# Four store buffers for layer 0's last latent tiles, and another start and pace for the row maxima of both layers

## The chip, the cores and the metric

The kernel runs on one core of one Trainium2 chip. The metric is the device time of one execution in microseconds (us), as the median of several runs. A profile of one further execution shows what every engine did: TensorE (PE, with its weight loads shown apart as PEld), VectorE (DVE), ScalarE (ACT), GpSimd (POOL), and the queues of DMAs, of which SP issues most.

## The reference

Two layers of a diffusion backbone over 2048 latent tokens and 256 context tokens (18 tiles of 128), width 1024, all in float32. Layer 0 is latent attention beside gated linear attention, layer 1 a 2-D neighbourhood attention over windows of 8 x 16 grid positions. Cut to what matters here:

```python
# layer 0 (even): one wide projection, then queries and keys out of low-rank latents
lat = split_cols(jnp.dot(h, w_in), EVEN_SPLITS)            # q_lat 768, kv_lat 256, k_rope 32, gates, B branch
q = rms_norm(rms_norm(q_lat) @ w_uq, q_gain); k = rms_norm([rms_norm(kv_lat) @ w_ukv, k_rope], k_gain)   # 8 heads x 96
o = softmax(q k^T * scale) v                                # over all tokens and the context
# layer 1 (odd): q, k, v, z = split(h @ w_in), 16 heads x 64
s_lat = q . k_window + bias;  s_ctx = q . k_ctx
p = softmax(concat([s_lat, s_ctx]));  y = (p v * silu(z)) @ w_out
```

Both softmaxes subtract a row maximum. The kernel computes these maxima in a pass of its own, ahead of the attention.

## The kernel before

Products are kept at float32 accuracy by splitting each operand into a high and a low part and adding three matmuls: one *step* of a product over the width is three matmuls, and a *cell* (one tile of 128 tokens by one block of weight columns) has eight steps.

The program is written as Python that traces instructions in an order of priority. A planner then puts them into the fixed order of each engine's queue, by its own estimate of times, of data dependences and of when buffers come free. `issue_after(x)` makes everything traced inside it stand behind instruction `x` on `x`'s engine. A tile is named by a tag, and the tag has a number of buffers; a new tile of the tag waits until the oldest one's last reader is done. Pools that are opened later take the space of pools that are closed, and each of their tiles waits for the readers of what lay there.

**Layer 0, latent tiles** (`even_latent`, L436 and on). A loop over 18 tiles runs, each with an offset: `prep` and `gemm` (latent projection), `up` (queries and keys out of the latents) and `fin` (L582 to L599). `fin` takes a tile's queries (`z` = 0) and keys (`z` = 1) in two halves `h2` of four heads: four transposes into a bank `tp`, then ACT writes the high part and DVE the low part into a tile `qkhl` with two buffers, and SP stores it to DRAM with three DMAs (L597 twice, L598 once). Beside it, `ada_steps` computes modulation rows with the tags `adac0`, `adac1` (one buffer each) and `adaw` (two buffers); its sixteen parts are used up before tile 14 comes to `fin`. During the last tiles, `first` already computes some cells of the next stage, and weights of the next stage are loaded (`wraw`, L422) and split (`W...`, `wr1`) on ACT and DVE.

**Layer 0, the rest of the projection** (`even_rest`). 86 cells, 688 steps, run from the last tile to the first. `maxes` runs beside them: for each of 8 heads it loads the keys (`mk`, L685 and L686) and queries (`mq`), multiplies and takes maxima with DVE (L698, L699). That is 664 pieces of side work. Two of the weights that the cells need are loaded and split in the first 32 steps.

`weave(main, side, ratio, lag, head)` interleaves the two: after `head` steps of main work it draws `ratio` pieces of side work per step, and each main step is put behind the side piece that is `lag` pieces back. So side work may fall behind by `lag` pieces, and no more:

```python
        due, done, over = -float(head * ratio), [], 0.0
                n = len(done) - lag - 1 + int(over)
                if n >= 0:
                    es.enter_context(self.tc.issue_after(done[min(n, len(done) - 1)].ins))
```

**Layer 1, values and gates** (`odd_vz`). 65 cells, 520 steps; beside them `maxes` for 16 heads of 16 query blocks each, 256 pieces: two matmuls into banks `mx` (five of them), POOL's two additions to a head's bias table `mtab`, and DVE's additions with a running maximum (L1689 to L1702). This `maxes` already loads its keys behind the last weight load (`wload`).

**Layer 1, attention** (`odd_attention`). Its loads are one chain on SP (`load`, L113: each behind the one before), in this order: queries of the odd head, first keys, values, two bias tables, context keys, queries of the even head (`q`, needed by the first scores), second keys, context values, mask, and so on. Their tiles lie in the space of the stage before: the first queries in that of `mk` and `mtab`, the values in that of `mtab`, the keys, tables and even queries in that of the last weights of `odd_vz`, the mask in that of its activations.

Of the kernel before, what the change touches and what calls it, by code (L numbers as in the profile page):

```python
# [10 lines left out]
F32 = mybir.dt.float32  # L11
F32R = mybir.dt.float32r
# [5 lines left out]
P = 128  # L18
# [5 lines left out]
NT = T // P  # L24
# [3 lines left out]
A_HEADS, A_NOPE, A_ROPE, A_V = 8, 64, 32, 64  # L28
A_QK = A_NOPE + A_ROPE
# [59 lines left out]
class Kern:  # L89
# [346 lines left out]
    def even_latent(self, ws, wrest, kept):  # L436
        nc, tc = self.nc, self.tc
# [5 lines left out]
        with ExitStack() as es:  # L443
# [3 lines left out]
            with ExitStack() as es2:  # L447
# [4 lines left out]
                hi, lo = win[0] = [self.tl(ws, [P, KD, LAT_CHUNK], "W0" + z, F32R, bufs=1) for z in "hl"]  # L452
# [8 lines left out]
            sp = self.pool(es, "esA", bufs=2, side="left", reuse_waits="tile")  # L461
# [120 lines left out]
            def fin(t):  # L582
                qn, kn = nat.pop(t)
                for z, (src, da, dc) in enumerate(((qn, self.QA, self.QC), (kn, self.KA, self.KC))):
                    col = 2 * z + (0 if t < NCT else 1)
                    for h2 in range(2):
                        ps = self.tl(pp, [P, 4, P], "tp")
                        for j in range(4):
                            nc.tensor.transpose(ps[:A_QK, j, :], src[:, h2 * 4 + j, :], self.ident[:])
                        hl = self.tl(sp, [P, 4, 2, P], "qkhl", F32R, bufs=2)  # L590
                        hi, lo = hl[:A_QK, :, 0, :], hl[:A_QK, :, 1, :]
                        self.act(hi, ps[:A_QK], AF.Copy, scale=qkg[:A_QK, col : col + 1])
                        nc.vector.scalar_tensor_tensor(out=lo, in0=ps[:A_QK], scalar=qkg[:A_QK, col : col + 1],
                                                       in1=hi, op0=ALU.mult, op1=ALU.subtract)
                        hs, ts = slice(h2 * 4, h2 * 4 + 4), slice(t * P, t * P + P)
                        for part in range(2):
                            nc.sync.dma_start(da[part, hs, :, ts].rearrange("h d t -> d h t"), hl[:A_NOPE, :, part, :].bitcast(F32))  # L597
                        nc.sync.dma_start(dc[hs, :, :, ts].rearrange("h s d t -> d (h s) t"),  # L598
                                          hl[A_NOPE:A_QK].rearrange("d h s t -> d (h s) t").bitcast(F32))  # L599

            ada = self.ada_steps([(0, 4), (0, 5)] + [(1, b) for b in range(6)], sp, pp, "tp")

# [39 lines left out]
    def even_rest(self, ws, win, hT):  # L642
        nc = self.nc
        self.zaT = self.scr("zaT", (4, P, T), F32)
        self.x1 = self.scr("x1", (T, D), F32)
        with ExitStack() as es:
            wp = self.pool(es, "ewB", side="left", reuse_waits="tile")
            sp = self.pool(es, "esB", bufs=2, side="left", reuse_waits="tile")
            pp = self.pool(es, "epB", bufs=2, space=PSUM, reuse_waits="tile")
            self.ahead += [self.held(self.rest_steps(win, 0, ws, "WU")), self.rest_steps(win, 1, wp, "wr1")]  # L650

            def cell(t, j):
                hi, lo = hT[t]
                wh, wl = win[j]
                w = self.REST[j]
                ps = self.tl(pp, [P, 512], "gm")
                yield from self.mm3_steps(ps[:, :w], (lambda k: hi[:, k, :], lambda k: lo[:, k, :]),
                                          (lambda k: wh[:, k, :], lambda k: wl[:, k, :]), range(KD))
                u = self.tl(sp, [P, 512], "u", bufs=4)
                if j < 2:  # L660
                    self.last_tanh = self.act(u[:], ps[:], AF.Tanh, scale=0.5)
                    nc.vector.scalar_tensor_tensor(out=u[:], in0=u[:], scalar=1.0, in1=ps[:], op0=ALU.add, op1=ALU.mult)
                else:
                    self.act(u[:, :w], ps[:, :w])
                if j == 0:
                    pt = self.tl(pp, [P, 4, P], "tp", bufs=1)
                    for b in range(4):
                        nc.tensor.transpose(pt[:, b, :], u[:, b * P : b * P + P], self.ident[:])
                    z = self.tl(sp, [P, 4, P], "zt")
                    self.act(z[:], pt[:])  # L670
                    nc.gpsimd.dma_start(self.zaT[:, :, t * P : t * P + P].rearrange("j p t -> p j t"), z[:])
                elif j == 1:
                    st = nc.gpsimd.dma_start(self.Un[t, :, 1056:], u[:])
                    with self.tc.issue_after(st.ins):
                        nc.gpsimd.dma_start(self.x1[t * P : t * P + P, :], self.i["xin"][t * P : t * P + P, :])
                else:
                    nc.gpsimd.dma_start(self.Un[t, :, (j - 2) * 352 : (j - 1) * 352], u[:, :352])

            cells = self.cells(list(range(NT))[::-1], (2, 3, 4, 0, 1), lambda t, j: j not in (2, 3) or t < NT - 2)
            gemms = self.stream(cells, hT, cell, lambda t: self.reload(0, t))  # L680

            def maxes():
                for h in range(A_HEADS):
                    k = self.tl(sp, [P, T], "mk", F32R, bufs=2)
                    nc.sync.dma_start(k[:A_NOPE].bitcast(F32), self.KA[0, h])  # L685
                    nc.sync.dma_start(k[A_NOPE:A_QK].bitcast(F32), self.KC[h, 0])  # L686
                    m = self.tl(sp, [P, NT, 5], "mm")
                    nc.vector.memset(m[:], -3e38)
                    for t in range(NT):
                        if t % 6 == 0:  # L690
                            q = self.tl(sp, [P, 768], "mq", F32R)
                            nc.sync.dma_start(q[:A_NOPE].bitcast(F32), self.QA[0, h, :, t * P : t * P + 768])
                            nc.sync.dma_start(q[A_NOPE:A_QK].bitcast(F32), self.QC[h, 0, :, t * P : t * P + 768])
                        lim = CTX if t < NCT else T
                        for n, k0 in enumerate(range(0, lim, 512)):
                            w = min(512, lim - k0)
                            ps = self.tl(pp, [P, 512], "mx", bufs=5)
                            mm = nc.tensor.matmul(ps[:, :w], q[:A_QK, (t % 6) * P : (t % 6) * P + P], k[:A_QK, k0 : k0 + w], start=True, stop=True)  # L698
                            nc.vector.tensor_reduce(out=m[:, t, n : n + 1], in_=ps[:, :w], axis=AX.X, op=ALU.max)  # L699
                            yield mm  # L700
                    mc = self.tl(sp, [P, NT], "mc", bufs=1)
                    nc.vector.tensor_reduce(out=mc[:], in_=m[:], axis=AX.X, op=ALU.max)
                    ps = self.tl(pp, [P, 512], "mx", bufs=5)
                    mm = nc.tensor.transpose(ps[:NT, :P], mc[:], self.ident[:])
                    r = self.tl(sp, [P, P], "mr", F32R, bufs=1)
                    self.act(r[:NT], ps[:NT, :P], AF.Copy, scale=-1.0)
                    nc.gpsimd.dma_start(self.QM[h].rearrange("(t p) -> t p", p=P), r[:NT].bitcast(F32))
                    yield mm

            self.weave(gemms, maxes(), 1.06, 30, 20)  # L710

    @staticmethod
    def back_order():
# [899 lines left out]
    def odd_vz(self, ws, win, hT):  # L1613
        nc = self.nc
# [3 lines left out]
        with ExitStack() as es:  # L1618
            sp = self.pool(es, "osB", bufs=2, side="left", reuse_waits="tile")
# [93 lines left out]
            first = [NT - 3, NT - 2, NT - 1]  # L1713
            cells = self.cells(first + list(range(NT - 3))[::-1], (4, 5, 6, 7), lambda t, j: (j > 4 or t < NT - 3) and (j < 6 or t >= NCT))
            gemms = self.stream(cells, hT, cell, lambda t: self.reload(1, t))
            self.weave(gemms, maxes(), 0.57, 15, 32)


    def odd_attention(self, out, right, left, wout):
# [508 lines left out]
```

## Time and profile before

| | |
|---|---|
| median of 3 runs | 3563.59 us (3560.05 to 3564.49) |
| the profiled execution | 3565.63 us, of which the span of its instructions 3563.9 us |
| mean granted PE clock | 0.984 |
| busy: PE, DVE, ACT, POOL | 97%, 68%, 41%, 35% of the span |
| moved by DMA | 526.75 MB, mean 148 GB/s |

A line of the profile's timeline has the start, the duration, the engine, the line of the program, the operation, what it writes from what it reads, and a count; at its end stands how long the engine was idle before it and what ended that. A row of the windows view has a stretch of time, its length, each engine's busy time with a count of instructions, the granted clock of PE as a share, the mean busy share of the DMA engines, and GB/s. Busy PE time is not PE at its peak: where the granted clock is 0.5, the same matmul takes about twice as long.

### The profile page before, as it was taken

To read this page: it belongs to the slowest core of one execution; us is meant where nothing else is said; L and a number is where in the kernel's file an instruction comes from. 1 tells how busy PE (TensorE), PEld (TensorE's weight loads), DVE (VectorE), ACT (ScalarE), POOL (GpSimd) and SP (SyncE) were. 2 spreads that over 40 slices of the span, in tenths; PEclk is the share of its full clock that TensorE was granted. 3 is DMA by queue.
4 is the path that set the end of the run, shared out by engine and by line. 5 is a ranking of instruction groups with operands and counts; after the bars stand their busy time and mean duration, and the time that the engine had idled before them with its cause. 6 is when DMAs were issued, how large, how long until landed. Compare 5 with 4: busy or idle time off the path is not lost. (4 is left out here: it accounts for less than half of the span.)

```text
span 3563.9 us, 54063 instructions
## 1 busy us (share of the span) xinstructions
PE 3453.2 (97%) x19460; PEld 2666.8 (75%) x19460; DVE 2431.0 (68%) x4798; ACT 1449.8 (41%) x2647; POOL 1243.9 (35%) x1400
## 2 busy tenths in 40 slices
PE   7999999999999999999999999999999997999999
PEld 6888987888896666665557878888788885556577
DVE  4677756888885777768876655444477874666875
ACT  5445542111113554546664354544322222555532
POOL 1333431111111333422211144334234443888852
PEclk9999999999999999999999999999999998999999
DMA  7555555232315242334525765445744447888684
GB/s 253 144 158 157 152 141 152 91 107 93 102 65 165 62 133 80 103 116 132 176 79 142 144 193 151 134 138 164 244 139 159 155 152 183 206 223 219 192 234 79
DMA packets 379596, 526.75 MB, mean 148 GB/s; under 512 B 34633, under 2 KB 254233, under 8 KB 372882
## 3 DMA queue, kind: packets, MB, share of 16 engines
q1 hardware_dynamic: 326450, 405.32, 39.3%
q0 software_dynamic: 29856, 82.14, 9.2%
q10 hardware_dynamic: 23024, 35.85, 3.0%
q8 instruction: 154, 2.52, 0.3%
q14 instruction: 112, 0.92, 0.1%
HBM read 344.39 MB, written 196.60 MB: 152 GB/s over the span
## 5 line engine op out<-in xcount | busy, mean ns | idle before, releaser
L699 DVE TENSOR_REDUCE mm<-mx 128x1 f32<-128x512 f32 (+1 forms) x656 | 388.3, 627 | 82.5 <-PE mx L698 75.5
L108 ACT ACTIVATE apt<-st 128x1024 f32<-128x1024 f32 (+1 forms) x296 | 300.0, 1014 | 313.2 <-PE st L1168 298.0
L1175 DVE TENSOR_TENSOR acc<-acc,apt 128x1024 f32<-128x1024 f32 x256 | 340.6, 1330 | 80.6 <-ACT apt L108 61.5
L1168 PE MATMUL st<-aq,akh 64*128 64x512 f32 x1728 | 313.9, 411 | 1.1 <-ACT apt L108 0.8
L1078 PE MATMUL av<-apt,av 128*64 128x512 f32 x1152 | 265.8, 598 | 0.0
L1945 DVE TENSOR_TENSOR opt<-st,tab 128x64 f32<-128x64 f32 (+10 forms) x576 | 144.2, 315 | 151.0 <-PE st L1787 67.6
L1826 POOL TENSOR_TENSOR oacc<-oacc,opt 128x576 f32<-128x576 f32 (+5 forms) x192 | 223.3, 1186 | 39.2 <-ACT rl L108 19.6
L698 PE MATMUL mx<-mk,mq 96*128 96x512 f32 (+1 forms) x656 | 236.0, 373 | 0.5 <-DVE mm L699 0.5
L1168 PE MATMUL st<-aq,akl 64*128 64x512 f32 (+1 forms) x1152 | 231.4, 393 | 0.0
L1702 DVE CUSTOM_DVE_ANT_1 mx<-mx,mtab 128x217 f32<-128x217 f32 (+12 forms) x576 | 183.6, 339 | 53.3 <-PE mx L1696 40.6
L108 ACT ACTIVATE u<-gm 128x352 f32<-128x352 f32 (+1 forms) x140 | 68.4, 496 | 370.9 <-PE gm L133 208.5
L1168 PEld LDWEIGHTS st<-aq,akh 64*128 64x128 f32 x1728 | 154.1, 187 | 83.6 <-ACT apt L108 28.0
L1078 PEld LDWEIGHTS av<-apt,av 128*64 128x64 f32 x1152 | 76.2, 136 | 135.3 <-issue 134.3
L108 ACT ACTIVATE opt<-opt 128x930 f32<-128x930 f32 (+8 forms) x130 | 104.5, 805 | 108.6 <-DVE opt L1945 104.2
L698 PEld LDWEIGHTS mx<-mk,mq 96*128 96x128 f32 x656 | 121.2, 188 | 12.9 <-DVE mm L699 1.6
L1168 PEld LDWEIGHTS st<-aq,akl 64*128 64x128 f32 (+1 forms) x1152 | 112.6, 186 | 24.2
L1691 DVE TENSOR_REDUCE mm<-mx 128x2 f32<-128x512 f32 x128 | 88.3, 690 | 46.1 <-PE mx L1689 45.0
L220 POOL TENSOR_TENSOR oss<-oss,mhalf 128x8 f32<-128x8 f32 x68 | 113.3, 1666 | 5.0
L131 PE MATMUL gm<-w1h,hhi 128*128 128x512 f32 x280 | 112.2, 401 | 0.0
L133 PE MATMUL gm<-w1h,hlo 128*128 128x512 f32 x280 | 110.3, 394 | 0.0
L1786 PE MATMUL st<-q,kt 128*128 128x480 f32 (+5 forms) x256 | 99.5, 391 | 11.1 <-DVE opt L1945 8.1
L132 PE MATMUL gm<-w1l,hhi 128*128 128x512 f32 x280 | 110.0, 393 | 0.0
(694 smaller groups left out, 9743.9 us busy)
## 6 DMA issues: line engine op xcount, KB each, us to landing
q<-Q SPq DMA_DIRECT2D x48, 512.0 KB
H<-x ACTq DMA_DIRECT2D x32, 512.0 KB
adaw<-ada_w SPq DMA_DIRECT2D x64, 256.0 KB
wraw<-w_od SPq DMA_DIRECT2D x64, 256.0 KB
K1t<-okt POOLq DMA_DIRECT2D x32, 512.0 KB, 10.1
kt<-K1t SPq DMA_DIRECT2D x32, 512.0 KB
x<-H SPq DMA_DIRECT2D x31, 512.0 KB
mtab<-rpb_q SPq DMA_DIRECT2D x16, 899.0 KB
```

Of the source, the lines that this page charges most:

```text
L108: return self.nc.scalar.activation(out, in_, func, **kw)
L131: self.nc.tensor.matmul(out, lh(k), rh(k), start=start and j == 0, stop=False)
L133: yield self.nc.tensor.matmul(out, ll(k), rh(k), start=False, stop=stop and j == n - 1)
L220: return g.tensor_tensor(out=out, in0=out, in1=self.mhalf[:, : shp[1]], op=ALU.pow)
L698: mm = nc.tensor.matmul(ps[:, :w], q[:A_QK, (t % 6) * P : (t % 6) * P + P], k[:A_QK, k0 : k0 + w], start=True, stop=True)
L699: nc.vector.tensor_reduce(out=m[:, t, n : n + 1], in_=ps[:, :w], axis=AX.X, op=ALU.max)
L1078: mm = nc.tensor.matmul(O[j, nb][i * 64 : i * 64 + 64, :w], V[j, kt // TT][:, kt % TT, i * 64 : i * 64 + 64], pts[:, i, :w], start=n == 0, ...
L1168: mm = nc.tensor.matmul(ps[:, o // 64, :w], k[o : o + r, kb, kq], Q[o : o + r, qb, :w], start=m == 0, stop=m == 4)
L1175: added = nc.vector.tensor_tensor(out=acc[:, :, :w], in0=a[:, :, :w], in1=pts[:, :, :w], op=ALU.add)
L1702: nc.vector.tensor_tensor_reduce(out=s, in0=s, in1=tb[:, ri : ri + rn, ci : ci + cn], scale=1.0, scalar=-3e38, op0=ALU.add, op1=ALU.max, a ...
L1826: self.psum = nc.gpsimd.tensor_tensor(out=a, in0=a, in1=pts[:, :, a0 - r0 : a1 - r0, :], op=ALU.add)
L1945: bias = nc.vector.tensor_tensor(out=pt[:, d[0], d[1]], in0=ps[:, d[0], d[1]], in1=tabs[j][i][:, ri : ri + rn, ci : ci + cn], op=ALU.add)
```

## The change

Three things are changed.

- In `fin`, for the tiles 14 to 17, the second half of the heads (`h2` = 1) no longer takes a `qkhl` buffer. Its two parts go to tiles of their own: for the queries (`z` = 0) `adac0` and `adac1`, for the keys (`z` = 1) the two buffers of `adaw`. The sizes are the same. Such a half is stored with four DMAs and not three, since its parts no longer lie beside each other.
- Layer 0's weave starts the maxima after 36 steps (20 before) at 1.09 pieces a step (1.06 before), with the same lag of 30. Each head's key loads stand behind the weight load traced last.
- Layer 1's weave draws 0.615 pieces a step (0.57 before), with the same lag of 15 and the same head of 32.

```diff
@@ fin, in even_latent
-                        hl = self.tl(sp, [P, 4, 2, P], "qkhl", F32R, bufs=2)
-                        hi, lo = hl[:A_QK, :, 0, :], hl[:A_QK, :, 1, :]
+                        if t < NT - 4 or h2 == 0:
+                            hl = self.tl(sp, [P, 4, 2, P], "qkhl", F32R, bufs=2)[:A_QK]
+                            hi, lo = hl[:, :, 0, :], hl[:, :, 1, :]
+                        else:
+                            tags = [("adaw", 2)] * 2 if z else [("adac0", 1), ("adac1", 1)]
+                            hi, lo = [self.tl(sp, [P, 4, P], a, F32R, bufs=n)[:A_QK] for a, n in tags]
...
-                        for part in range(2):
-                            nc.sync.dma_start(da[part, hs, :, ts].rearrange("h d t -> d h t"), hl[:A_NOPE, :, part, :].bitcast(F32))
-                        nc.sync.dma_start(dc[hs, :, :, ts].rearrange("h s d t -> d (h s) t"),
-                                          hl[A_NOPE:A_QK].rearrange("d h s t -> d (h s) t").bitcast(F32))
+                        for part, y in enumerate((hi, lo)):
+                            nc.sync.dma_start(da[part, hs, :, ts].rearrange("h d t -> d h t"), y[:A_NOPE].bitcast(F32))
+                            if t >= NT - 4 and h2:
+                                nc.sync.dma_start(dc[hs, part, :, ts].rearrange("h d t -> d h t"), y[A_NOPE:].bitcast(F32))
+                        if t < NT - 4 or h2 == 0:
+                            nc.sync.dma_start(dc[hs, :, :, ts].rearrange("h s d t -> d (h s) t"),
+                                              hl[A_NOPE:].rearrange("d h s t -> d (h s) t").bitcast(F32))
@@ maxes, in even_rest
-                    nc.sync.dma_start(k[:A_NOPE].bitcast(F32), self.KA[0, h])
-                    nc.sync.dma_start(k[A_NOPE:A_QK].bitcast(F32), self.KC[h, 0])
+                    with self.tc.issue_after(self.wload.ins):
+                        nc.sync.dma_start(k[:A_NOPE].bitcast(F32), self.KA[0, h])
+                        nc.sync.dma_start(k[A_NOPE:A_QK].bitcast(F32), self.KC[h, 0])
@@ end of even_rest
-            self.weave(gemms, maxes(), 1.06, 30, 20)
+            self.weave(gemms, maxes(), 1.09, 30, 36)
@@ end of odd_vz
-            self.weave(gemms, maxes(), 0.57, 15, 32)
+            self.weave(gemms, maxes(), 0.615, 15, 32)
```

## The prediction

> **What bounds the kernel now.** I read the page first, then the busy time of the engines stretch by stretch, then, wherever TensorE (PE) was not full, its timeline with what ended each pause.
>
> ```profile
> span 3563.9 us, 54063 instructions
> PE 3453.2 (97%) x19460; PEld 2666.8 (75%) x19460; DVE 2431.0 (68%) x4798; ACT 1449.8 (41%) x2647; POOL 1243.9 (35%) x1400
> ```
>
> PE is busy 97% of the span, so time is won only where PE pauses, or runs at the lower clock that follows a pause: 3563.9 - 3453.2 = 110.7 us of pauses in all. Inside the two stages with row maxima there are none to win. In the next view (window, then PE, weight loads, DVE, ACT, POOL busy, then granted clock, DMA share, GB/s) the first two rows are layer 1's weave, as a whole and at its densest for VectorE (DVE); the third is its end, the fourth the change to the odd attention.
>
> ```profile
> 2600.00:2950.00 350.00, 350.00 (x1733) 293.94 (x1732) 269.19 (x1144) 91.38 (x154) 156.07 (x136) 1.00 0.48 152
> 2724.00:2736.00 12.00, 12.00 (x62) 10.04 (x61) 11.31 (x51) 2.82 (x5) 2.57 (x1) 1.00 0.70 244
> 2952.00:2976.00 24.00, 24.00 (x121) 20.17 (x120) 19.30 (x83) 6.95 (x11) 5.14 (x8) 1.00 0.22 69
> 2979.00:3003.00 24.00, 6.22 (x28) 4.70 (x26) 0.00 (x0) 1.46 (x3) 4.50 (x8) 0.70 1.07 261
> ```
>
> PE is full for all 350 us of the weave; what fails is the handoff. DMA is almost idle just before it (0.22) and saturated after it (1.07) while PE does nothing. Layer 0's handoff, from the latent tiles to the rest of the projection, pauses too. The PE timeline has the long pauses:
>
> ```profile
> 516.16 1.12 PE L535 MATMUL tp<-ident,u 128*128 128x128 f32 x4 [3.64 <-DVE qkhl L593]
> ...
> 545.34 1.91 PE L589 MATMUL tp<-ident,kn 128*96 128x128 f32 x8 [3.77 <-DVE qkhl L593]
> 559.39 0.80 PE L131 MATMUL gm<-WUh,hhi 128*128 128x512 f32 x1 [4.03 <-ACT u L108]
> ```
> ```profile
> 519.07 0.69 PE L122 MATMUL up<-WUh,lth 128*128 128x384 f32 x1 [1.80 <-ACT lth L108]
> ```
> ```profile
> 3004.77 1.62 PE L1786 MATMUL st<-q,kc 128*128 128x512 f32 x3 [19.55 <-DMA q<-Q]
> ```
>
> And the clock after each pause, in the windows view again:
>
> ```profile
> 516.10:524.00 7.90, 6.04 (x21) 5.55 (x22) 4.08 (x12) 1.76 (x3) 2.98 (x3) 0.50 0.59 143
> 545.30:548.00 2.70, 2.66 (x12) 2.62 (x13) 0.55 (x1) 0.97 (x1) 0.00 (x0) 0.50 1.07 276
> 559.30:568.00 8.70, 8.61 (x27) 6.79 (x28) 0.94 (x1) 0.39 (x2) 1.34 (x2) 0.67 1.00 281
> 1099.30:1105.00 5.70, 5.52 (x42) 4.55 (x44) 0.01 (x1) 2.77 (x4) 1.81 (x5) 0.70 1.06 340
> 3004.70:3024.00 19.30, 18.06 (x48) 10.84 (x50) 6.75 (x26) 7.23 (x12) 8.61 (x5) 0.53 1.03 267
> ```
>
> Busy time times (1 - clock) is what the low clock costs: 3.0, 1.3, 2.8, 1.7 and 8.5 us. So layer 0's three pauses are worth at most 3.64 + 1.80 + 3.0 = 8.4, 3.77 + 1.3 = 5.1 and 4.03 + 2.8 = 6.8 us, and the layer 1 handoff at most 19.55 + 8.5 = 28 us.
>
> **Part 1, four sets of store buffers (tiles 14 to 17).** Before, a latent tile's four evictions share two `qkhl` buffers, so the third and fourth wait until the first two have been stored. ScalarE (ACT) shows it for the tile at 514:
>
> ```profile
> 514.22 0.68 ACT L108 ACTIVATE qkhl<-tp,qkg 96x512 fp32r<-96x512 f32 x1 [2.32 <-DMA QC<-qkhl]
> 517.86 0.68 ACT L108 ACTIVATE qkhl<-tp,qkg 96x512 fp32r<-96x512 f32 x1 [2.96 <-DMA QC<-qkhl]
> ```
> ```profile
> 515.36 0.74 DVE L593 SCALAR_TENSOR_TENSOR qkhl<-tp,qkg,qkhl 96x512 fp32r<-96x512 f32 x1
> ```
>
> Now each eviction has its own buffer. The third starts at 514.22 - 2.32 = 511.9, the fourth right behind it at 512.6 in place of 517.86. DVE's second half of the third, which at 515.36 + 0.74 hands PE its bank back, ends about 2.3 earlier, and `lth`, queued on ACT behind the fourth, moves from 518.4 to 513.9 (its transposes, at about 513.9, hold it to 514.6). So the matmul of 519.07 starts about 4.0 earlier, and some 1.4 of the 5.4 us pause stays. Does the clock still fall? The row at 1099.30 is the nearest: it runs at 0.70 and loses 1.7 us. I take 1.7 as what stays, so 3.0 - 1.7 = 1.3 is won: this pause gives 4.0 + 1.3 = 5.3 us (bounds 0 and 8.4).
>
> The pause ahead of that row was 1.46 us, the length that I expect to stay at 516:
>
> ```profile
> 1099.36 0.50 PE L1168 MATMUL st<-aqc,akh 64*128 64x256 f32 x4 [1.46 <-DVE u L662]
> ```
>
> The Trainium skill (TensorE: Matmul & The Clock Gate, What's actually happening) says that the clock halves only after an idle window of about 3.4 us. By that rule a pause of 1.4 us would cost no clock and the sum would be 1.7 us better; the trace does not agree, since the clock was half for 0.30 x 5.7 / 0.5 = 3.4 us behind only 1.46 us of pause, so the measured loss stays.
>
> The other two pauses are not buffer waits in this trace. At 545 the evictions stand behind weight splits on DVE, at 559 `u` stands behind a weight that is still loading:
>
> ```profile
> 542.17 2.36 DVE L426 TENSOR_TENSOR WUl<-wraw,WUh 128x1024 fp32r<-128x1024 f32 x2 [3.18 <-ACT WUh L108]
> 544.45 1.40 DVE L593 SCALAR_TENSOR_TENSOR qkhl<-tp,qkg,qkhl 96x512 fp32r<-96x512 f32 x2
> ```
> ```profile
> 557.93 1.06 ACT L108 ACTIVATE wr1h<-wraw 128x1024 fp32r<-128x1024 f32 x1 [2.66 <-DMA wraw<-w_rest]
> 558.89 0.80 ACT L108 ACTIVATE u<-gm 128x352 f32<-128x352 f32 x2
> ```
>
> That order was laid down by the planner when two buffers held the evictions back; with four it may put them first, which DVE needs 0.7 us for and not 2.36 + 1.40. Bounds 0 and 5.1 + 6.8 = 11.9; I take 3, a quarter, since nothing in the trace forces the order to change.
>
> What it adds: the odd half of each tile stores four times and not three, 2 x 4 = 8 more stores on SP.
>
> ```profile
> L598 SPq DMA_DIRECT2D KC<-qkhl x36: 425/602/972, 116.4 to 556.3; - x36
> ```
>
> 8 x 0.60 = 4.8 us of SP's queue, in which the weight loads stand, but spread over four tiles, 1.2 us each; SP no longer stands in wait for evictions, which covers it. Bare, the last tile's 1.2 us would delay the last weights: nothing on PE until 1.2 us of slack are gone. I cost it at 0. Layer 0 thus gives 5.3 + 3 = 8.3 us.
>
> **Part 2, layer 0's maxima from step 36 at 1.09, first keys behind the weights.** A step is three matmuls. Maxima lag by 30 of theirs, so 664 of them end at step 20 + 664/1.06 + 30/1.06 = 674.7 of 688 before, and 36 + 664/1.09 + 30/1.09 = 672.7 now: 2 steps of 0.7 us, 1.4 us earlier at the handoff (bounds 0 and 3). The price is early: sixteen steps run without some 17 maxima between them, so PE needs the second weights 17 x 0.2 = 3.4 us sooner. Before, two weight loads stand behind the keys on SP:
>
> ```profile
> 557.09 0.50 SPq L685 DMA_DIRECT2D mk<-KA  x1
> ...
> 560.73 0.59 SPq L422 DMA_DIRECT2D wraw<-w_rest  x1
> ```
>
> Passing them ahead of the keys returns those 560.73 - 557.09 = 3.6 us, and the keys have sixteen steps of 0.7 = 11 us more. Both cancel: 0, and up to 3.4 us lost if the order fails.
>
> **Part 3, layer 1's maxima at 0.615.** Same head (32), same lag (15). The 256 query blocks end at step 32 + 256/0.57 + 15/0.57 = 507 of 520 before; the trace agrees, the last one starting 8.3 us, 12 steps of 0.70, ahead of the last cell's end at 2985.2 (matmuls 0.235 us apart):
>
> ```profile
> L1696 PE MATMUL mx<-mk,mz x256: 280/328/495, 2556.7 to 2976.5; 128*128 128x360 f32 x32, 128*128 128x480 f32 x32, 128*128 128x264 f32 x16, 128*128 128x352 f32 x16
> ```
> ```profile
> 2984.83 0.39 PE L133 MATMUL gm<-w1h,hlo 128*128 128x512 f32 x1
> ```
>
> Now they end at 32 + 271/0.615 = 473, 47 steps or 33 us ahead: at 2952 on the old scale. This matters because SP's loads for the odd attention are one chain, and its first lies in the space of the last keys:
>
> ```profile
> 2976.87 1.72 SPq L113 DMA_DIRECT2D q<-Q  x3
> ...
> 2992.10 1.88 SPq L113 DMA_DIRECT2D q<-Q  x3
> ...
> 2999.81 0.54 SPq L113 DMA_DIRECT2D maskk<-maskk  x1
> ```
>
> The chain starts at 2976.87, as the last maximum ends. The second group of queries is what PE waits for at 3004.77; ahead of it and with it go 6.3 MB by the tile sizes in the code (queries 3.1, keys 1.2, values 1.0, tables 1.0), 27.6 us, 228 GB/s. The parts in the space of maxima can now start at 2952, those in the space of the last 32-KB weights when these are done, four or five cells of 5.6 us before the end (2957 to 2963). From 2957, with the first 1.1 MB moved, 5.2 MB take 23 us: the queries land about 2980, and PE finds them.
>
> Next late is the mask. Its load follows the last context values, which are stored after the last cell, and the tables are masked by GpSimd (POOL) before DVE may use them:
>
> ```profile
> 2986.15 0.59 POOL L1607 DMA_DIRECT2D V1c<-ovz  x1 [0.23 <-ACT ovz L108]
> ```
> ```profile
> 3012.04 4.73 POOL L1783 TENSOR_TENSOR tab<-tab,maskk 128x1034 f32<-128x1034 f32 x2 [24.34 <-PE st L1787]
> ```
> ```profile
> 3014.46 1.16 DVE L1945 TENSOR_TENSOR opt<-st,tab 128x32 f32<-128x32 f32 x6 [36.02 <-POOL tab L1783]
> ```
> ```profile
> V1c<-ovz POOLq DMA_DIRECT2D x4, 256.0 KB, 5.2
> ```
>
> 2986.15 + 5.2 = 2991.4; the mask issues at 2992.5 and lands in about 4 (0.5 MB at 228 GB/s and some latency, an estimate), and half of POOL's 4.73 brings DVE's first bias to 2999. That is 15 us before 3014.46, and behind the bias the order is the same: **15 us** won, not 28, the rest staying as a pause of some 6 us with its slow clock. Bounds: 6 if the stores and loads crowd each other (the chain's 2999.81 - 2986.15 - 5.2 = 8 us repeated), 22 if the context scores and sums fill the mask's wait.
>
> The denser pace costs DVE nothing on average: a query block now takes (2976.5 - 2556.7)/256 = 1.64 us, of it 1.75 steps x 0.70 = 1.23; with 1.63 steps it takes 1.55. DVE's 269.19/350 = 77% becomes 81%. The densest stretch, 11.31 of 12, becomes 99.9%, so I take 1 us of pauses (0 to 24, below).
>
> **The sum.** 8.3 + 1.4 + 15 - 1 = 23.7 us. The profiled execution took 3565.63 (its span 3563.9 and 1.7 around it): 3541.9. The median of the runs, 3563.59, lies 2.0 below it, so I forecast **3540**.
>
> **Rivals.** *DVE becomes the bound.* If the dense stretches cannot go at 1.55 us a block and the weave keeps 1.64, PE pauses 256 x 0.09 = 24 us, many times a few tenths, with the clock loss of the handoff kept (8.5): 3540 + 24 + 8.5 = 3572, slower. It decides from 0.1 us of pause per block on. For it: 11.31 of 12. Against: 77% mean, and five banks between the engines. 9%.
> *The loads do not move.* The planner keeps the chain where it was, or DMA is held elsewhere: part 3 gives 0, 3540 + 15 = 3555. For it: the order is the planner's. Against: the chain began the moment its space was free. 13%.
> *Layer 0 keeps its pauses*, the weights or keys being late in turn: 3540 + 8.3 = 3548. For it: two of three pauses come from order, not buffers. 17%.
> *It does not do what it says:* both orders stay or new pauses eat the gain: 3564. 6%.
>
> **Numbers.** My forecast has 55%. 0.2%, 7 us, is about what a measurement of this kernel can tell from no change, so faster means below 3556.5: 55 + 17 + 13 = 85%; same 6%, slower 9%. The range reaches down to 3540 - 8 (layer 0) - 7 (handoff) - 3 = 3522 and up past the two half gains to 3558.
>
> **What would show it.** Right: no DMA wait ahead of `qkhl` on ACT from 480 us on; the 3.64 us pause near 516 gone; the last `mx` matmul some 33 us before the last `gm`; SP's first `q` load there; the 19.55 us pause below 8; DVE's first bias about 14 us after the last cell, not 29. Wrong: pauses on PE in the weave with DVE `mx` as releaser, or the `q` loads still beginning as the cells end.

## The result, and the profile after

Over six runs of each, the changed kernel took 3545.22 us (3541.9 to 3550.34) against 3564.04 us before (3557.59 to 3567.88). The ratio is 0.995, 95% interval 0.9936 to 0.9965: 18 us faster, where 23.7 were forecast. The forecast time of 3540 lies 5 us below the median, inside the range of 3522 to 3558. The profiled execution is the slowest of the six (3550.34 us). Executions of one kernel differ by up to 10 us within these six, so in what follows stages are compared, not positions on the whole span.

The page of the kernel after: its first line, and the engines' busy times.

```profile
span 3548.3 us, 54039 instructions
...
PE 3449.7 (97%) x19460; PEld 2665.7 (75%) x19460; DVE 2434.6 (69%) x4798; ACT 1451.1 (41%) x2647; POOL 1243.6 (35%) x1400
```

The same matmuls take nearly the same busy time; PE's pauses shrank from 110.7 to 3548.3 - 3449.7 = 98.6 us. Now PE's timeline after, at the pauses that the prediction priced:

```profile
514.13 1.11 PE L535 MATMUL tp<-ident,u 128*128 128x128 f32 x4 [3.64 <-DVE qkhl L597]
515.93 0.69 PE L122 MATMUL up<-WUh,lth 128*128 128x384 f32 x1 [0.69 <-ACT lth L108]
...
541.48 1.92 PE L589 MATMUL tp<-ident,kn 128*96 128x128 f32 x8 [3.77 <-DVE qkhl L597]
557.30 0.79 PE L131 MATMUL gm<-WUh,hhi 128*128 128x512 f32 x1 [4.66 <-ACT u L108]
...
2990.91 0.96 PE L1794 MATMUL st<-q,kc 128*128 128x512 f32 x3 [0.69 <-ACT ovz L108]
...
2993.49 0.50 PE L1794 MATMUL st<-q,kc 128*128 128x512 f32 x1 [0.45 <-ACT opt L108]
...
3001.67 0.66 PE L1794 MATMUL st<-q,kt 128*128 128x384 f32 x1 [4.12 <-DVE opt L1953]
```

Layer 0's pauses of 3.64 and 3.77 us are there to the hundredth; only the 1.80 has become 0.69. The pause of 4.03 us before, at 559, is 4.66 now. At the handoff of layer 1 the 19.55 us are gone; three pauses of together 5.26 us stand in their place, and the last of them has a new releaser, the biased scores. The windows behind four of these places, after (granted clock third from the end):

```profile
514.10:521.90 7.80, 7.08 (x30) 6.59 (x31) 4.38 (x11) 1.19 (x2) 2.94 (x3) 0.66 0.57 157
541.50:544.20 2.70, 2.70 (x12) 2.63 (x13) 0.69 (x2) 1.29 (x2) 0.00 (x0) 0.50 0.99 299
1103.00:1108.70 5.70, 5.54 (x54) 4.28 (x55) 0.41 (x1) 3.83 (x6) 1.86 (x5) 1.00 1.11 382
2990.20:3009.50 19.30, 13.89 (x49) 7.35 (x48) 6.76 (x26) 7.40 (x13) 8.74 (x6) 0.82 0.96 267
```

By the prediction's measure (busy x (1 - clock)) the handoff's slow clock fell from 8.5 to 13.89 x 0.18 = 2.5 us. With the pauses that is 19.55 - 5.26 + 8.5 - 2.5 = 20.3 us won at this one place. Why it was won stands in the row of the maxima and in SP's timeline after:

```profile
L1704 PE MATMUL mx<-mk,mz x256: 280/328/492, 2562.2 to 2956.6; 128*128 128x360 f32 x32, 128*128 128x480 f32 x32, 128*128 128x264 f32 x16, 128*128 128x352 f32 x16
```
```profile
2956.97 1.72 SPq L113 DMA_DIRECT2D q<-Q  x3
...
2979.76 1.76 SPq L113 DMA_DIRECT2D q<-Q  x3
...
2992.18 0.56 SPq L113 DMA_DIRECT2D maskk<-maskk  x1
```

The last maximum stands 33.2 us ahead of the last cell's matmul at 2989.84 (8.3 before, 2976.5 against 2984.83), and the chain starts 0.4 us behind it, as it did before. The queries have landed when PE comes to them: what ends its first pause, of 0.69 us, is ACT and no longer a load.

### The profile page after: what moved, and what is told of

Read it like the earlier page. It is cut to its first block, busy times and chain, and to the rows that moved or that the text cites. A ratio compares the mean times of both kernels' runs of the same rounds, so it can differ in the third digit from the quotient of the medians.

```text
span 3548.3 us, 54039 instructions
## 1 busy us (share of the span) xinstructions
PE 3449.7 (97%) x19460; PEld 2665.7 (75%) x19460; DVE 2434.6 (69%) x4798; ACT 1451.1 (41%) x2647; POOL 1243.6 (35%) x1400
## 5 line engine op out<-in xcount | busy, mean ns | idle before, releaser
L1710 DVE CUSTOM_DVE_ANT_1 mx<-mx,mtab 128x217 f32<-128x217 f32 (+14 forms) x576 | 182.4, 340 | 35.8 <-PE mx L1704 25.5
```

Of the source, the lines that this page charges most:

```text
L1710: nc.vector.tensor_tensor_reduce(out=s, in0=s, in1=tb[:, ri : ri + rn, ci : ci + cn], scale=1.0, scalar=-3e38, op0=ALU.add, op1=ALU.max, a ...
```

## The experiments

Each was timed against the kernel before on the same chip, in three batches (names with e, f and g; f on another chip than e and g). Across batches the ratios to before are compared, not the times. "Base" is the kernel after with layer 0's maxima left as they were (20 steps, 1.06, keys not held).

**The three parts apart.** Three kernels with one part each, and one without part 2.

```diff
 # e1_stores: only the new store buffers in fin
 # e2_maxima0: only layer 0's weave and its keys
+            self.weave(gemms, maxes(), 1.09, 30, 36)
 # e3_maxima1: only layer 1's weave
+            self.weave(gemms, maxes(), 0.615, 15, 32)
 # e4_no_maxima0 ("base"): the kernel after, layer 0's weave and keys as before
-            self.weave(gemms, maxes(), 1.09, 30, 36)
+            self.weave(gemms, maxes(), 1.06, 30, 20)
```

> Only the store buffers are changed; maxima of both layers as before. Theory (layer 1's handoff is the whole gain, layer 0's two edits cancel or lose): the 3.64 us pause ahead of the transposes of u stays, because DVE, not the buffer, sets it; the pause ahead of the up matmuls shrinks from 1.80 to about 0.7; the time is 0 to 3 us below before (about 3562), not the 8.3 us of the prediction. Rival (the prediction's step holds when layer 0's maxima are left alone): 3.64 gone or halved, 6 to 9 us below before, about 3556.

> Only layer 0's maxima are changed (36 steps, 1.09, keys behind weights). Theory: pauses of 1 to 2 us on PE ahead of the transposed row maxima (mx from ident and mc) at the ends of some heads, since DVE is fuller, and the time 2 to 6 us above before (3566 to 3570). Rival (the pauses in the changed kernel's weave came from the stores' new order or from chance): no such pauses, and 0 to 2 us below before, as predicted (1.4).

> Only layer 1's pace is changed (0.615). Theory: the 19.55 us pause shrinks to under 1 us, one of about 4 us stays where the first scores of the window wait for DVE's bias, and the time is 18 to 21 us below before (3543 to 3546). Rival (the prediction's term): 15 us, 3549. Rival (the gain needs layer 0's edits too): under 12 us.

> The changed kernel with layer 0's maxima put back (20 steps, 1.06, keys not held): stores and layer 1's pace changed. Theory: 4 us faster than the changed kernel, about 3541 against before's 3564. Rival (layer 0's maxima gain 1.4 as predicted): 1 to 2 us slower than the changed kernel, 3547.

| kernel | median us | ratio to before (95%) | worth |
|---|---|---|---|
| stores alone | 3558.98 | 0.9990 (0.9981 to 0.9998) | -4 us |
| layer 0's maxima alone | 3572.37 | 1.0019 (1.0009 to 1.0029) | +7 us |
| layer 1's pace alone | 3544.02 | 0.9943 (0.9931 to 0.9955) | -20 us |
| base | 3542.32 | 0.9936 (0.9922 to 0.9950) | -23 us |

The three add up to -17, and the whole change measured -18: within what these runs can tell, the parts do not interact. In all four the stated theory came out, within the intervals; the rivals did not, the prediction's 15 us for layer 1 among them. Layer 1's pace is the gain, and part 2 is a loss that hides in the total. Where it is lost shows in PE's waits from 570 to 1090 us. In base the view lists no wait of PE in this stretch, in the kernel before one of 0.5 us, and none of either is at a head's end. The kernel with layer 0's maxima alone, and then the kernel after, have this one:

```profile
PE mx L705 <- DVE mc L703: 5.0, 3, 2.3
```
```profile
PE mx L712 <- DVE mc L710: 4.3, 3, 2.3
```

`mc` is the reduction that closes a head; PE transposes its result. One such place in the kernel after, PE's timeline and then DVE's:

```profile
716.19 0.28 PE L712 MATMUL mx<-ident,mc 128*18 128x128 f32 x1 [1.66 <-DVE mc L710]
```
```profile
712.11 3.74 DVE L707 TENSOR_REDUCE mm<-mx 128x1 f32<-128x512 f32 x7
715.88 0.25 DVE L710 TENSOR_REDUCE mc<-mm 128x18 f32<-128x90 f32 x1
```

DVE is busy without a gap, with seven reductions in a row ahead of the one that closes the head; the transpose needs them all. The kernel with part 2 alone also shows the price that the prediction had named for the sixteen steps without maxima: PE comes too early to the cells of the late weights.

```profile
567.55 0.50 PE L131 MATMUL gm<-WUh,hhi 128*128 128x512 f32 x1 [2.03 <-ACT u L108]
```

5.0 + 2.03 us lie within the measured loss of 7 us (3 to 10 by its interval).

**Which piece of part 2.** The pace alone and the keys alone, on base.

```diff
 # f1_pace109
-            self.weave(gemms, maxes(), 1.06, 30, 20)
+            self.weave(gemms, maxes(), 1.09, 30, 20)
 # f2_keys20: key loads inside issue_after(self.wload.ins), weave (1.06, 30, 20)
```

> Stores and layer 1's pace as changed; layer 0's maxima start at step 20 as before but run at 1.09 pieces a step, keys not held. Theory A (the pace is what costs: DVE, at 84% to 88% in this weave, falls behind, and the transposed row maxima at the heads' ends wait on PE): the pauses ahead of mx from mc of 1 to 2.3 us at three or four heads' ends are there, and the time is 4 to 6 us above the same kernel with 1.06, about 3546 to 3547. Theory B (the late start costs, since the weights come before the maxima and DVE gets all of them later): no such pauses, within 1.5 us of the kernel with 1.06, about 3542.

> The changed kernel with layer 0's maxima from step 20 at 1.06 again, but with the keys still held behind the weight load traced last. Theory A (the pace costs): equal to the kernel without the hold, 3541 to 3543, no pauses at the heads' ends; the pause ahead of the first cell with the second gate weights moves by under 1 us. Theory C (the hold costs, since later heads' keys too queue behind a weight load): 3546 or more, with PE waiting for mx from mk.

Measured: 3542.15 us, ratio 0.9945 (0.9931 to 0.9958), and 3542.74 us, 0.9938 (0.9926 to 0.9951), against 0.9936 of base. Keys held behind the weights cost nothing that can be measured, and PE's waits list 0.2 us there. With 1.09 alone the time cannot be told from base, and so does not decide between theories A and B; but PE already waits at the heads' ends, more often and for less long than theory A had it:

```profile
PE mx L711 <- DVE mc L709: 2.9, 6, 0.9
```

The stretch from the first cell after the third pause (559.39 before) to the first attention score (1099.36 before) took 541.6 us there. In base it took 538.7, and in the five other kernels with base's layer 0 537.6 to 538.9. So the pace makes some 3 us in this stage. The kernel after took 545.7 there, and part 2 alone 547.7 (540.0 before). What is beyond the pace comes with the start at step 36, alone or together with the held keys; I did not run that by itself.

**What holds layer 0's pauses.** The prediction took the second pause for the planner's order. On base, the two high parts of the last tile's queries were put ahead of the weight splits on ACT, by the program's own `issue_after`:

```diff
+                        e = self.act(hi, ps[:A_QK], AF.Copy, scale=qkg[:A_QK, col : col + 1])
+                        if t == NT - 1 and z == 0:
+                            self.evicted = e
 # f4_evict_first; in the kernel as it is, held() traces loads and splits of weights so:
             with self.tc.issue_after(self.evicted.ins):
```

> Stores and layer 1's pace as changed, layer 0's maxima as before; the last tile's two query evictions on ACT now stand ahead of the weight splits of the next stage. Theory (the 3.77 us pause is the planner's order, not buffers): it falls under 1.5 us; if nothing is late in turn, 3 to 5 us below the kernel without this, about 3538. Rival (the weights are what the stage waits for in the end): the pause of 7.38 us ahead of the first cell with the gate weights grows by what the other lost, time unchanged at 3542 or above.

Measured: 3536.82 us, ratio 0.9925 (0.9911 to 0.9938), the fastest kernel of the study. DVE's timeline, first of the kernel after, then of this one:

```profile
538.32 2.36 DVE L426 TENSOR_TENSOR WUl<-wraw,WUh 128x1024 fp32r<-128x1024 f32 x2 [2.94 <-ACT WUh L108]
540.59 0.74 DVE L597 SCALAR_TENSOR_TENSOR qkhl<-tp,qkg,qkhl 96x512 fp32r<-96x512 f32 x1
```
```profile
536.20 0.75 DVE L599 SCALAR_TENSOR_TENSOR qkhl<-tp,qkg,qkhl 96x512 fp32r<-96x512 f32 x1 [2.65 <-ACT qkhl L108]
536.86 0.74 DVE L599 SCALAR_TENSOR_TENSOR adac<-tp,qkg,adac 96x512 fp32r<-96x512 f32 x1
537.72 2.36 DVE L426 TENSOR_TENSOR WUl<-wraw,WUh 128x1024 fp32r<-128x1024 f32 x2
```

And PE's timeline and the clock behind the pause, of this kernel:

```profile
537.09 1.21 PE L589 MATMUL tp<-ident,kn 128*96 128x128 f32 x8 [1.21 <-DVE qkhl L599]
```
```profile
537.10:539.80 2.70, 2.70 (x19) 2.50 (x20) 2.58 (x3) 2.68 (x4) 0.00 (x0) 1.00 0.83 166
```

The pause is 1.21 us in place of 3.77 and the clock stays full: 2.56 + 1.35 = 3.9 us. The stretch from the transposes behind the first pause to the cell behind the third fell from 43.4 us in base to 38.9. Order held this pause, not buffers. The rival did not come about: the pause behind it is 5.04 us, where base has 7.38. In the six kernels with base's layer 0 the stretch took 42 to 44 us. Against base the medians' intervals overlap, so the 4 us are shown by the stage, not by the time.

**What holds layer 1's remaining pause.** Two theories for the 4.12 us: the mask's load comes late (it stands behind the context values), or POOL's order puts the masked tables behind its first sums, `oacc`. POOL's timeline, after:

```profile
2996.03 2.49 POOL L1816 TENSOR_TENSOR oacc<-opt 128x512 f32<-128x512 f32 x2 [4.33 <-ACT opt L108]
2998.49 4.69 POOL L1791 TENSOR_TENSOR tab<-tab,maskk 128x1034 f32<-128x1034 f32 x2
```

```diff
 # f3_mask_first: base, the mask's load traced ahead of the first context values
+            self.load(mk[:], self.i["maskk"].rearrange("p (r c) -> p r c", r=NR))
             values_ctx(0, V[0])
-            self.load(mk[:], self.i["maskk"].rearrange("p (r c) -> p r c", r=NR))
 # g3_pool_mask: f3, and POOL's first sums behind its masked tables
-                        with self.tc.issue_after(bias.ins):
+                        with self.tc.issue_after(bias.ins), self.tc.issue_after(self.masked.ins) if j == 0 else ExitStack():
```

> Stores and layer 1's pace as changed, layer 0's maxima as before; in the odd attention's chain of loads the mask now stands ahead of the first context values. Theory (what is left of the handoff is the mask, queued behind context values that are stored only after the last cell): DVE's first bias moves 4 to 5 us nearer to the last cell, the 4.12 us pause goes under 1 us, and the time is 3 to 6 us below the kernel without the swap, about 3537. Rival (the bias waits for the tables or for POOL, not for the mask's place in the chain): pause and time unchanged, 3542.

> Stores and layer 1's pace as changed, layer 0's maxima as before; the mask ahead of the first context values in the chain, as in the run that moved nothing, and POOL's two masked tables ahead of its first sums of context scores. Theory (with the mask's load moved, POOL's order is what holds the bias: 2.49 us of sums stand ahead, themselves behind ACT): the first bias comes 4 to 5 us nearer to the last cell, the 4.12 us pause falls under 1 us, and the time is 3 to 5 us lower, about 3537. Rival (ACT's exponentials of the context scores, or the half clock after the handoff, hold PE anyway): pause gone but time within 1.5 us of 3541.

Measured: 3539.59 us, ratio 0.9934 (0.9921 to 0.9946), and 3539.5 us, 0.9934 (0.9922 to 0.9946); base 0.9936. Neither can be told from base. Moving the load in the chain moved it little: in base it goes out 1.3 us behind the end of the last cell (2985.52 against 2984.20), with the load first right at that end (2981.39 against 2981.36), since the mask's tile lies in the space of the stage's activations, which the last cell still reads. The pause is 4.12 us again, and POOL goes from `oacc` (2987.16) straight to the tables. With POOL's order turned as well, SP, POOL, PE and the windows view of that kernel show the other condition:

```profile
2979.16 0.35 SPq L113 DMA_DIRECT2D maskk<-maskk  x1
```
```profile
2987.61 4.70 POOL L1790 TENSOR_TENSOR tab<-tab,maskk 128x1034 f32<-128x1034 f32 x2 [7.02 <-DMA maskk<-maskk]
```
```profile
2990.80 0.66 PE L1793 MATMUL st<-q,kt 128*128 128x384 f32 x1 [4.36 <-DVE opt L1952]
```
```profile
2979.20:2987.60 8.40, 6.18 (x24) 3.82 (x24) 0.00 (x0) 4.58 (x9) 0.54 (x1) 1.00 0.90 265
```

Half a megabyte now needs 8.4 us from issue to use, at a DMA share of 0.90, and it arrives when POOL would have been done with `oacc` anyway. Both theories are half right: two waits end together, and taking one away shows the other. The kernel at pace 0.70, below, has neither wait, and there the pause is short.

**How dense the pace can be.** On base, a sparser and a denser pace.

```diff
 # g1_pace0585
+            self.weave(gemms, maxes(), 0.585, 15, 32)
 # g2_pace070
+            self.weave(gemms, maxes(), 0.70, 15, 32)
```

> Stores as changed, layer 0's maxima as before, layer 1's pace 0.585, between before's 0.57 and the change's 0.615. Theory (what the handoff costs is set by when the last maximum frees the space of the chain's first load): the last mx comes 32 + 271/0.585 = 495 steps in, 25 steps or 17 us ahead of the last cell, 9 us earlier than at 0.57, so PE's pause at the handoff is 9 us shorter, about 10.5 us, and the time lies half way, about 3551 (at 0.57 3559, at 0.615 3542). Rival (any pace above 0.57 is enough, or the gain comes from another order of the loads): pause under 2 us and 3543.

> As the run before with 0.70. Theory: the last mx comes 101 steps, 71 us ahead, but the loads in the space of the last weights still wait, and the first scores already found their queries at 0.615, so nothing more is won at the handoff; DVE is asked for 77% x 1.64/1.41 = 90% on average and for 110% in its densest stretch, so PE pauses in the weave ahead of mx or of the cells' transposes, 3 to 10 us in all: 3545 to 3552. Rival (DVE keeps up, the banks smooth it out): no pauses, 3542.

Measured: 3553.45 us, ratio 0.9976 (0.9967 to 0.9985), and 3546.34 us, 0.9963 (0.9949 to 0.9976). The first is clear of base's interval (0.9922 to 0.9950); the second's just touches it, and its loss is shown by the stage. At 0.585 the maxima's row and PE's timeline are:

```profile
L1703 PE MATMUL mx<-mk,mz x256: 282/328/496, 2553.4 to 2963.7; 128*128 128x360 f32 x32, 128*128 128x480 f32 x32, 128*128 128x264 f32 x16, 128*128 128x352 f32 x16
```
```profile
2994.20 1.62 PE L1793 MATMUL st<-q,kc 128*128 128x512 f32 x3 [12.70 <-DMA q<-Q]
```

From the last maximum to the first scores it takes 2994.20 - 2963.7 = 30.5 us; before it took 3004.77 - 2976.5 = 28.3. The theory held: 12.70 us of pause where 10.5 were forecast. So PE finds its queries when the maxima end some 30 us ahead of the last cell; 0.585 gives 17 us, 0.615 gives 33, and nothing between was run. At 0.70 they end 77 us ahead (2915.2 against 2992.3), and the weave itself takes longer, as the windows view, PE's waits and one row of ACT of that kernel show:

```profile
2560.00:2915.00 355.00, 350.57 (x1747) 294.68 (x1746) 306.56 (x1334) 94.75 (x160) 165.91 (x137) 1.00 0.48 155
```
```profile
PE gm L131 <- ACT ovz L108: 3.8, 1, 3.8
PE tp L1649 <- DVE ovz L1646: 2.6, 2, 2.0
PE mx L1703 <- DVE mm L1698: 0.7, 2, 0.5
```
```profile
2984.19 0.60 ACT L108 ACTIVATE ozt<-tp 128x512 f32<-128x512 f32 x1 [13.51 <-DMA z<-ozt]
```

The weave with its last cells took 440.6 us against 428.5 in base. DVE is at 306.56/355 = 86% while the maxima run, and PE waits for it some 4 us in all; this is the prediction's rival "DVE becomes the bound", in a mild form, somewhere between 0.615 and 0.70. The longest single wait, 3.8 us, is not DVE's: it comes 70 us behind the last maximum, and ACT had stood 13.51 us for a store before it. Why that store took so long is not shown. Most of what is left of the 12 us is PE's busy time, 4 us more for the same matmuls.

The handoff itself got shorter at 0.70, which the theory did not expect. POOL and PE of that kernel:

```profile
2996.54 4.75 POOL L1790 TENSOR_TENSOR tab<-tab,maskk 128x1034 f32<-128x1034 f32 x2 [2.38 <-PE st L1794]
```
```profile
2999.78 0.42 PE L1793 MATMUL st<-q,kt 128*128 128x384 f32 x1 [0.93 <-DVE opt L1952]
```

Here the planner put the masked tables ahead of POOL's first sums, and the mask, issued at 2992.72, was there within 3.8 us, at a DMA share of 0.70 in that time. With both conditions away the pause of 4.12 us is 0.93. It does not make up for the weave.

**All together.** Base with the mask's load first, POOL's tables first and the evictions first.

```diff
 # g4_best: the edits of g3_pool_mask and f4_evict_first
```

> As the run before, with the last tile's query evictions also ahead of the weight splits on ACT. Theory (the two add up): about 4 us below the run before, 3533, a ratio to before of about 0.9915. Rival (layer 0's 4 us were chance): equal to the run before.

Measured: 3540.66 us, ratio 0.9942 (0.9929 to 0.9954). It did not add up: layer 0's stretch is short here too (39.9 us), yet the time is not below base. The intervals of the two overlap, so which of the two is faster stays open. By medians the fastest is the one with the evictions first alone: 27 us below before in its batch, and some 8 below the change as given.

## Why the prediction was right or wrong, point by point

**The bound** was right: PE pauses and the low clock behind them. The weave of layer 1 stayed full, the handoff was the place.

**Part 1, first pause: 5.3 us forecast, 3.64 us kept.** The failed step is "DVE's second half of the third ... ends about 2.3 earlier". With its own buffer ACT wrote the high part early and without a wait, but DVE did not follow. ACT's timeline after, then DVE's:

```profile
509.77 0.67 ACT L108 ACTIVATE qkhl<-tp,qkg 96x512 fp32r<-96x512 f32 x1
510.53 0.68 ACT L108 ACTIVATE adaw<-tp,qkg 96x512 fp32r<-96x512 f32 x1
```
```profile
511.20 0.96 DVE L568 TENSOR_TENSOR qn<-qn,sqk 128x768 f32<-128x768 f32 x1 [1.08 <-POOL sqk L220]
512.08 0.42 DVE L556 COPY vn<-up 128x256 f32<-128x256 f32 x1
512.41 0.68 DVE L572 TENSOR_REDUCE sqk<-sql 128x8 f32<-128x512 f32 x1
513.00 0.42 DVE L517 TENSOR_TENSOR rx<-qn,grow 128x256 f32<-128x256 f32 x1
513.34 0.74 DVE L597 SCALAR_TENSOR_TENSOR qkhl<-tp,qkg,qkhl 96x512 fp32r<-96x512 f32 x1
```

`qkhl` is the fifth of a row of instructions that DVE runs without a gap, and the first of them waits for POOL's `sqk`. Before, DVE ran the same five in the same order, behind the same wait:

```profile
513.23 0.96 DVE L568 TENSOR_TENSOR qn<-qn,sqk 128x768 f32<-128x768 f32 x1 [1.07 <-POOL sqk L220]
```

I had quoted the row of the eviction before, at 515.36, without what stands ahead of it in DVE's queue: the row names no releaser, so DVE was busy right up to it, and ACT was not what held it. ACT's buffer wait of 2.32 us was real and off the path. Only the second wait, for the fourth eviction, went: 1.80 to 0.69. With the clock (7.08 x 0.34 = 2.4 in place of 3.0) this pause gave 1.1 + 0.6 = 1.7 us, in the bounds of 0 to 8.4.

**Part 1, the other two: 3 us forecast, nothing shown.** The order stayed (3.77 again), and the third pause, 4.66, varies from 3.85 to 7.38 us between six kernels with the same layer 0 (base's). That order held the second was right, as the kernel with the evictions first showed; that four buffers would change the order was a guess, and wrong. The stores alone measured -4 us, interval -0.7 to -7, of which 1.7 are this first pause. The profiles suggest that the rest lies ahead of layer 0's attention, but name no pause for it: the first score starts at 1093.8 to 1097.2 us in the six kernels with the new stores and base's maxima, and at 1098.9 and 1099.4 in the two with the old stores (before, and layer 1's pace alone), 4 us apart on average.

**Part 2: 1.4 us of gain forecast, +7 measured alone.** The bounds (0 to 3 of gain, up to 3.4 of loss) do not hold the 7, and its interval, 3 to 10, only reaches their edge. The sum counted steps and weights. It did not count that each head's end needs DVE to be level, at a pace that brings more reductions per step. The 2.03 us at the weights is the price that was named; "Passing them ahead of the keys returns those ... 3.6 us" is the step that failed there. The keys did go behind the weights, but four loads of queries, which are not held, stood there in their place. SP's timeline of the kernel with part 2 alone:

```profile
556.43 0.50 SPq L693 DMA_DIRECT2D mq<-QA  x1
...
558.82 0.94 SPq L422 DMA_DIRECT2D wraw<-w_rest  x2
```

The splits of the two weights begin 9.0 and 11.9 us behind the first cell after the third pause there, and 9.3 and 11.9 before. So the weights came no earlier, while PE needed them earlier.

**Part 3: 15 - 1 forecast, 20 measured.** The mechanism was right up to the queries: the maxima end 33 us ahead, the chain starts with them, and PE finds the queries. What remains was mis-sized: "some 6 us with its slow clock" was right for the pauses (5.26), but the slow clock fell from 8.5 to 2.5 us with them. And the first bias came earlier than forecast, as DVE's timeline after shows:

```profile
3000.87 1.17 DVE L1953 TENSOR_TENSOR opt<-st,tab 128x32 f32<-128x32 f32 x6 [30.78 <-POOL tab L1791]
```

It comes 11 us behind the last cell, where 14 were forecast and 29 measured before. The step that failed here is "Its load follows the last context values, which are stored after the last cell". POOL's last store of context values and SP's first load of them, after:

```profile
2991.15 0.54 POOL L1615 DMA_DIRECT2D V1c<-ovz  x1 [4.95 <-ACT ovz L108]
```
```profile
2991.50 0.57 SPq L113 DMA_DIRECT2D ov<-V1c  x1
```

The load goes out 0.35 us behind the issue of that store, while such a store takes 5.2 us to land before and 7.0 after (medians); in base it goes out even ahead of it (2984.84 against 2985.12). In the code this first load reads only the first half of the columns, whose last store is two cells older. So the mask is issued 2.0 us behind the end of the last cell, where the forecast had 2992.5 - 2985.2 = 7.3. From there to the first bias it took 8.7 us, with 6.5 forecast: the tables began 6.3 us behind the mask's issue and not 4, with POOL's first sums ahead of them. The two errors partly cancel.

The denser pace cost nothing, with 1 us forecast: from the first maximum to the end of the last cell 428.2 us against 428.9. Two small slips of arithmetic in this part change nothing: DVE's densest stretch comes to 99.7% and not 99.9%, and 256 x 0.09 is 23 us and not 24.

**The sum** came within 5 us because part 3 gave 6 us more while layer 0 gave 13 less (a gain of 9.7 forecast with part 2; a gain of 4 and a loss of 7 measured). That these errors had opposite signs was luck. Of the rivals, "layer 0 keeps its pauses" (3548) comes nearest to what layer 0 did, but the reason it names, weights or keys late in turn, explains only the 2.03 us of part 2.

## What to carry to other kernels

Before an early buffer is costed as a gain, read the whole queue ahead of the instruction that hands the resource back: where an eviction's row names no releaser, its engine was busy right up to it, and here no buffer moved it. Side work that frees the space of the next stage's loads should end as far ahead of the stage's end as that load chain is long (some 30 us here, read off as last side matmul to first use) and not much denser: at 0.70 the handoff still gained, but the weave lost 12 us, a third of it in waits for DVE. Where several edits go in together, time them apart: a loss of 7 us lay unseen in a gain of 18.

## What the runs showed of the hardware

The same pause does not always cost the clock. The 1.46 us ahead of layer 0's attention stand in all fourteen profiles; behind them the clock stayed full in ten (1.00 in the window from 1103.00 after), and was half for some 3.4 us in four (a mean of 0.70 in the prediction's window from 1099.30 before, and likewise in `e3_maxima1`, `f3_mask_first` and `f4_evict_first`), with no tie to the code (base and `f3_mask_first` have the same layer 0). So the prediction's loss of 1.7 us behind such a pause was one draw of two outcomes. Behind the 19.55 us pause before, the clock stayed at half for some 18 us, though PE was busy 18.06 of 19.3 us by the profile (0.53 in the prediction's window from 3004.70). The Trainium skill (TensorE: Matmul & The Clock Gate, What's actually happening) says that the window in which activity is judged runs freely, so that a change of clock depends on where the work falls in it; these draws agree with that, while four drops behind 1.46 us disagree with its rule that at least one idle window of about 3.4 us goes ahead of a drop.
